# Strassen's scheme in the input projection of a hybrid decoder step: seven block products for eight, weight sums on GpSimd, product sums on VectorE

## The chip, the cores and the metric

The kernel runs on one core of a Trainium2 chip. The metric is the device time of one launch in microseconds (us). The core's engines work side by side, each with a queue of its own: TensorE (PE in the rows; PEld is its weight load), VectorE (DVE), ScalarE (ACT), GpSimd (POOL) and SyncE (SP), which issues nearly all transfers.

## The reference, cut to what matters

One step of two decoder layers for 512 prompt tokens and 32 sample tokens, 544 columns in all. The change touches one product, `z = hn @ w_in`; the rest is what its columns feed.

```python
for l in range(2):
    hn = rmsnorm(x, norm_g)
    z = hn @ w_in                      # (544 x 1024) @ (1024 x 10080), split into gates, heads, ...
    y_conv = c_b * conv3(c_c * c_h)                    # branch 0
    y_hg   = rmsnorm(hgrn2(hg_q, hg_f, hg_i, S0))      # branch 1
    y_mla  = mla(q_lat, kv_lat, k_pe, cache)           # branch 2
    y_mem  = cross_attention(m_q, mem_k, mem_v)        # branch 3
    ys = stack(y_conv, y_hg, y_mla, y_mem) * silu(sg)
    merged = sum_n sigmoid(mg[n]) * (ys[n] @ w_bout[n])
    x = x + merged @ w_o
```

All is float32. The large products are done as three products each of rounded parts (high x high, high x low, low x high), where low is what rounding left over.

## The kernel before, in words

**Tiles.** Activations stand feature-major: 128 features on the partitions, 544 token columns, eight such blocks for the 1024 features. The normalised input is split by `xn_finish` into `Hh` and `Hl` (8 blocks x 544 columns each). The columns of `w_in` are cut into 79 tiles of 128 a layer. One tile of weights is a 128x1024 array (512 KB): eight 128x128 blocks, one for each feature block.

**Items.** The program is a list of items: four for each of the memory key and value weights, the 79 tiles of `w_in` (the key says which: `mg` is a merge gate, `sg` a branch gate, `hq`, `hf`, `hi` the heads of hgrn2), the branch projections `pj` (32 a layer), and the output product `wo` (8). For each item:

- `load` (L1503) issues the transfer of the weights into a tile `wr` on SyncE, two items ahead (three buffers);
- `conv` (L1510) splits them one item ahead: ScalarE writes the high part `wh`, VectorE the low part `wl = wr - wh`;
- `z_mm` (L359) issues 48 matmuls: 8 blocks x 3 products for each half of 272 columns, summed in PSUM in one of two tiles `big` of two banks;
- `evac` reads the PSUM sum and makes of it what the branch needs (`ev_mg` at L662, `ev_pj` at L672 and others).

**Lanes.** Two generators run beside this: `lane_a` (memory attention, then hgrn2 of four heads) and `lane_b` (MLA of the prompt, then of eight samples). Each item makes one step of lane a after its first half and one of lane b at its end, so a lane's matmuls, its work on ScalarE and VectorE, and its gathers on GpSimd are spread over the items. They share 27 work tiles `t`, 128x544 each.

**What sets the order.** Instructions are written item by item, and a list scheduler with its own model of time puts them in order on each engine; each engine then works its queue strictly in that order and waits at the first instruction whose data or buffer isn't there. GpSimd's queue holds gathers of the paged cache (`in_lat`, `in_rop`), small copies, and the addition of a projection to the running sum (`e<-e`).

Of the kernel before, what the change touches and what calls it, by code (L numbers as in the profile page):

```python
# [19 lines left out]
P = 128  # L20
# [17 lines left out]
HG = ((2, 6), (0, 4))  # L38
NT = 27
PL = ()  # L40
PH = (2, 5)
LANE_PRI = {"a": 0, "b": 0, "mm": 0, "ev": 0, "cv": 0}
# [85 lines left out]

class Item:
    def __init__(self, key, l, src, n, mm, evac, pre=None):  # L130
        self.key, self.l, self.src, self.n = key, l, src, n
        self.mm, self.evac, self.pre = mm, evac, pre
        self.raw = self.hi = self.lo = None
# [3 lines left out]
def hybrid_kernel(ctx: ExitStack, tc: tile.TileContext, a, o):  # L137
# [5 lines left out]
    wrp = pool("wrp", 3)  # L143
    whp = pool("whp", 2)
    ep = pool("ep", 6)
# [4 lines left out]
    ssp = pool("ssp", 3)  # L150
    bigp = pool("bigp", 2, space=PSUM)
# [16 lines left out]
    big = lambda: bigp.tile([P, 2, 512], F32, tag="big", name="big")  # L168
# [45 lines left out]
    Rh = [kp.tile([P, 272], F32R, name=f"Rh{i}") for i in range(2)]  # L214
    Rl = [kp.tile([P, 272], F32R, name=f"Rl{i}") for i in range(2)]
# [21 lines left out]
    row4 = kp.tile([P, 4, P], F32R, name="row4")  # L237
    csq = kp.tile([P, T], F32, name="csq")

    def setup_first():  # L240
        V.memset(ones, 1.0)
        V.memset(epsc, EPS)
        x = t("b")[:, 0:4 * P].rearrange("p (h q) -> p h q", h=4)
        G.memset(x, 0.0)
        for h in range(4):
            G.memset(x[32 * h:32 * h + 1, h, :], 1.0)
        V.tensor_copy(row4, x)
        G.memset(cnew, 0.0)
        S.dma_start(out=gn, in_=a["gains"])

    def scale_rows(s1, s2):

        x = t("b")[:, 0:4 * NB]
        V.tensor_copy(x, row4i)
        ts(x, x, s1, s2, ALU.mult, ALU.add)
        V.tensor_copy(row4i, x)

    def setup():
        SY.dma_start(out=cst, in_=a["cst"])
        x = t("b")  # L260
# [98 lines left out]
    def z_mm(l, key):  # L359
        def run(it, half):  # L360
            if half == 0:
                it.ps = big()
            Hh, Hl = st[l]["H"]
            for k in range(KD):
                w = slice(k * P, (k + 1) * P)
                c = slice(half * HT, (half + 1) * HT)
                for n, (x, y) in enumerate(((it.hi, Hh), (it.hi, Hl), (it.lo, Hh))):
                    mm(it.ps[:, half, 0:HT], x[:, w], y[:, k, c], start=(k == 0 and n == 0), stop=(k == KD - 1 and n == 2))
        return run

    def proj_mm(l):
        def run(it, half):
            if half == 0:
                it.ps = big()
            yh, yl = st[l]["ys"]
            for k in range(4):
                w = slice(k * P, (k + 1) * P)
                c = slice(half * HT, (half + 1) * HT)
                for n, (x, y) in enumerate(((it.hi, yh), (it.hi, yl), (it.lo, yh))):
                    mm(it.ps[:, half, 0:HT], x[:, w], y[:, k, c], start=(k == 0 and n == 0), stop=(k == 3 and n == 2))  # L380
        return run

    def out_mm(l):
        def run(it, half):
            if half == 0:
                it.ps = big()
            Mh, Ml = st[l]["Ms"]
            if it.key[1] == 0:
                kh = [(k, hf) for k in range(KD) for hf in range(2)] if half == 0 else []
            else:  # L390
                kh = [(k, half) for k in range(KD)]
            for k, hf in kh:
                w = slice(k * P, (k + 1) * P)
                c = slice(hf * HT, (hf + 1) * HT)
                for n, (x, y) in enumerate(((it.hi, Mh), (it.hi, Ml), (it.lo, Mh))):
                    mm(it.ps[:, hf, 0:HT], x[:, w], y[:, k, c], start=(k == 0 and n == 0), stop=(k == KD - 1 and n == 2))
        return run

    def mem_mm(l, which, c):
        def run(it, half):  # L400
            if c == 0 and half == 0:
                st[l]["ps" + which] = big()
            it.ps = st[l]["ps" + which]
            mh, ml = st[l]["mn"]
            k = 2 * c + half
            w = slice(half * 512, (half + 1) * 512)
            for mt in range(2):
                m = slice((k % 2) * 256 + mt * P, (k % 2) * 256 + (mt + 1) * P)
                for n, (x, y) in enumerate(((mh, it.hi), (ml, it.hi), (mh, it.lo))):
                    mm(it.ps[:, mt, :], x[k // 2][:, m], y[:, w], start=(k == 0 and n == 0), stop=(k == KD - 1 and n == 2))  # L410
        return run

    def ps2(it):
        return it.ps[:, :, 0:HT]
# [17 lines left out]

    def xn_finish(l):
# [14 lines left out]
        Hh = kp.tile([P, KD, T], F32R, tag="H1", name="Hh")  # L448
        Hl = kp.tile([P, KD, T], F32R, tag="H2", name="Hl")
        st[l]["H"] = (Hh, Hl)  # L450
# [1219 lines left out]
```

## Time and profile before

| | |
|---|---|
| median of 3 runs | 1774.2 us (1771.57 to 1775.55) |
| the profiled execution | 1779.11 us |
| its span in the trace | 1777.3 us |
| TensorE busy | 1718.1 us, 14042 matmuls |
| VectorE busy | 1092.0 us, 2502 instructions |
| ScalarE busy | 863.9 us |
| GpSimd busy | 289.6 us |

Busy time of TensorE is the union of matmuls whose ends are modelled, so it hides short gaps between them; the spacing of matmuls in a dense stretch is the better measure. An instruction of VectorE is listed with its full duration, but the next one starts before it ends where neither waits, so start to start is what one costs in a full queue. Spans on GpSimd are rough. In the second layer the trace repeats the first nearly row by row.

### The profile page before, as it was taken

What the parts mean: (1) busy time and instruction counts of PE and PEld (TensorE: products, weight loads), DVE (VectorE), ACT (ScalarE), POOL (GpSimd) and SP (SyncE); (2) the same over time, 40 slices, a digit from 0 to 9 for tenths busy, and PEclk for the clock granted to TensorE, in tenths of its full rate; (3) what the DMA queues carried; (4) which work ended last, traced back from release to release, by engine and by line L of the source; (5) the groups of instructions that cost most, each with busy time, mean ns of one, the idle gap of its engine ahead of it and who ended that gap; (6) DMA issues with size and microseconds to landing.
All of it is one profiled execution on the core that took longest, in us unless ns stands there. A gap on an engine that the chain in (4) does not pass through costs nothing.

```text
span 1777.3 us, 36288 instructions
## 1 busy us (share of the span) xinstructions
PE 1718.1 (97%) x14042; PEld 1654.8 (93%) x14042; DVE 1092.0 (61%) x2502; ACT 863.9 (49%) x1659; POOL 289.6 (16%) x326
## 2 busy tenths in 40 slices
PE   6899999999998999999989999999999989999999
PEld 5899899999998999999969999999998989999999
DVE  7576554778676876334374656556877759753252
ACT  5646444565745663233246554356566465632231
POOL 3100000213232333100110100002131414221000
PEclk9999999999999999999989999999999989999999
DMA  6312632354344455433544235324444435554432
GB/s 225 116 60 69 208 111 83 121 158 152 112 148 140 142 173 158 145 128 108 158 142 123 60 122 187 98 72 152 151 127 140 155 92 171 169 152 145 147 108 99
DMA packets 129390, 236.79 MB, mean 133 GB/s; under 512 B 17025, under 2 KB 55298, under 8 KB 129218
## 3 DMA queue, kind: packets, MB, share of 16 engines
q1 hardware_dynamic: 121906, 213.45, 38.0%
q0 software_dynamic: 7168, 20.98, 4.0%
q8 instruction: 111, 1.82, 0.4%
q14 instruction: 61, 0.50, 0.1%
q10 hardware_dynamic: 144, 0.04, 0.0%
HBM read 204.55 MB, written 29.87 MB: 132 GB/s over the span
## 4 chain that ended last, share of the span: by engine, by line
PE 88%; ACT 5%; DVE 4%; issue 2%; DMA 1%; SPq 0%; DVEq 0%; ACTq 0%
PE big L171 67%; PE sm L171 19%; ACT L174 1%; ACT ta L174 1%; DVE wl L180 1%; ACT wh L174 1%; DVE e L177 1%; DVE ta L180 1%; ACT tb L174 1%; PE sm L1204 0%; PE sm L739 0%; PE sm L982 0%; DMA raw<-in_wk 0%; PE sm L1285 0%; PE sm L784 0%
## 5 line engine op out<-in xcount | busy, mean ns | idle before, releaser
L171 PE MATMUL big<-Hh,wh 128*128 128x272 f32 x2528 | 744.7, 295 | 4.2 <-ACT e L174 3.7
L171 PE MATMUL big<-Hh,wl 128*128 128x272 f32 x2528 | 739.2, 292 | 5.9 <-DVE wl L180 5.9
L171 PE MATMUL big<-Hl,wh 128*128 128x272 f32 x2528 | 734.4, 291 | 2.6 <-DVE Hl L180 2.6
L171 PEld LDWEIGHTS big<-Hh,wh 128*128 128x128 f32 x2528 | 478.9, 189 | 11.3 <-issue 4.6
L171 PEld LDWEIGHTS big<-Hh,wl 128*128 128x128 f32 x2528 | 478.1, 189 | 8.6 <-DVE wl L180 6.8
L171 PEld LDWEIGHTS big<-Hl,wh 128*128 128x128 f32 x2528 | 478.8, 189 | 7.3 <-DVE Hl L180 3.2
L174 ACT ACTIVATE wh<-wr 128x1024 fp32r<-128x1024 f32 (+1 forms) x248 | 235.0, 948 | 410.7 <-PE big L171 310.0
L180 DVE TENSOR_TENSOR wl<-wr,wh 128x1024 fp32r<-128x1024 f32 (+1 forms) x248 | 279.5, 1127 | 245.8 <-ACT wh L174 242.6
L174 ACT ACTIVATE tb<-sm 128x256 f32<-128x256 f32 (+6 forms) x380 | 137.1, 399 | 131.1 <-PE sm L171 100.1
L171 PE MATMUL big<-ysh,wl 128*128 128x272 f32 x512 | 148.3, 290 | 3.0 <-DVE wl L180 3.0
L171 PE MATMUL big<-ysh,wh 128*128 128x272 f32 x512 | 149.3, 292 | 0.0
L171 PE MATMUL big<-ysl,wh 128*128 128x272 f32 x512 | 148.6, 290 | 0.0
L180 DVE TENSOR_TENSOR ta<-ta 128x256 f32<-128x256 f32 (+3 forms) x248 | 110.0, 482 | 24.2 <-ACT ta L174 23.6
L171 PE MATMUL sm<-ta 128*128 128x128 f32 (+6 forms) x1424 | 124.4, 279 | 0.0
L174 ACT ACTIVATE ta<-ta 128x544 f32<-128x544 f32 (+3 forms) x180 | 94.8, 539 | 46.3 <-DVE ta L180 44.5
L171 PEld LDWEIGHTS sm<-ta 128*32 128x32 f32 (+1 forms) x1424 | 102.2, 147 | 8.8 <-issue 3.4
L171 PE MATMUL sm<-Rh,rb 128*128 128x272 f32 x512 | 109.7, 301 | 0.0
L189 DVE TENSOR_REDUCE s<-tb 128x8 f32<-128x512 f32 (+1 forms) x150 | 100.8, 673 | 13.2 <-ACT tb L174 12.9
L174 ACT ACTIVATE ta<-sm 128x512 f32<-128x512 f32 (+5 forms) x130 | 53.8, 429 | 99.3 <-PE sm L171 50.5
L171 PEld LDWEIGHTS big<-ysh,wl 128*128 128x128 f32 x512 | 96.4, 188 | 3.5 <-DVE wl L180 3.5
L180 POOL TENSOR_TENSOR e<-e 128x544 f32<-128x544 f32 x32 | 61.4, 1919 | 226.0 <-DVE e L177 186.9
L171 PEld LDWEIGHTS big<-ysh,wh 128*128 128x128 f32 x512 | 96.5, 189 | 1.0 <-issue 0.8
(236 smaller groups left out, 2564.8 us busy)
## 6 DMA issues: line engine op xcount, KB each, us to landing
wr<-in_w_in SPq DMA_DIRECT2D x158, 512.0 KB
wr<-in_wb SPq DMA_DIRECT2D x64, 256.0 KB
tb<-in_latT SPq DMA_DIRECT2D x256, 64.0 KB
md<-e SPq DMA_DIRECT2D x48, 272.0 KB
e<-md SPq DMA_DIRECT2D x32, 272.0 KB
ta<-in_mkT SPq DMA_DIRECT2D x32, 256.0 KB
ta<-in_mv SPq DMA_DIRECT2D x32, 256.0 KB
wr<-in_wo SPq DMA_DIRECT2D x16, 512.0 KB
```

The source lines that it names most:

```text
L171: return TE.matmul(out, lhsT, rhs, start=start, stop=stop)
L174: S.activation(out, in_, f, **k)
L177: V.scalar_tensor_tensor(out=out, in0=in0, scalar=sc, in1=in1, op0=op0, op1=op1)
L180: (eng or V).tensor_tensor(out=out, in0=in0, in1=in1, op=op)
L189: V.tensor_reduce(out=out, in_=in_, op=op, axis=AX.X, **k)
```

## The change

The 544 columns are cut in halves of 272, the 1024 features in halves of four blocks, and two tiles of weights are taken together, so that a pair is a product of 2x2 blocks. Strassen's scheme (in Winograd's form) makes it with seven block products. Each block product is 4 blocks x 3 products = 12 matmuls of 272 columns. 78 of a layer's 79 tiles go in 39 pairs; the tile `C` stays alone (`lone`).

- `xn_finish` writes seven blocks of the input (three as they are, four sums T1 to T4) in place of four: `Hh` and `Hl` grow from 8x544 to 7x4x272 columns.
- Of each pair's weights four blocks arrive by transfer (128x512 each), and **GpSimd** makes three more sums and one in place (`sums`, `after`): four additions of 128x512 a pair.
- All seven weight blocks are split into high and low, on ScalarE and VectorE as before, in pieces of 128x512 (`convert_to`).
- Each product lands in one PSUM bank of four. One is copied by ScalarE into a tile `uu`, and **VectorE** makes seven additions of 128x272 (PSUM plus SBUF into SBUF) that give the two results `z0`, `z1`. `evac` reads these from SBUF.
- Lane a steps after the second and the sixth product, lane b after the fourth and the seventh.
- Projections are read in halves (two instructions of 272 in place of one of 544). Loads run 11 block units ahead, sums 8, splits 4.
- To make room: 22 work tiles `t` for 27, 5 tiles `e` for 6, 2 softmax tiles `S` for 3, and smaller constants. The heads of hgrn2 start at other merge gates: `HG = ((2, 5), (0, 3))`.

```diff
-NT = 27
+HG = ((2, 5), (0, 3))
+NT = 22
-    wrp = pool("wrp", 3)
-    whp = pool("whp", 2)
-    ep = pool("ep", 6)
+    wrp = pool("wrp", 10)
+    whp = pool("whp", 4)
+    up = pool("up", 4)
+    ep = pool("ep", 5)
-    ssp = pool("ssp", 3)
-    bigp = pool("bigp", 2, space=PSUM)
+    ssp = pool("ssp", 2)
+    bigp = pool("bigp", 4, space=PSUM)
...
+    def three(u, out, rhs, first, last):
+        for k in range(4):
+            w = slice(k * P, (k + 1) * P)
+            yh, yl = rhs(k)
+            for n, (x, y) in enumerate(((u.hi, yh), (u.hi, yl), (u.lo, yh))):
+                mm(out, x[:, w], y, start=(first and k == 0 and n == 0), stop=(last and k == 3 and n == 2))
...
+    def pair(l, k0, k1, ev0, ev1, pre=None, psy=None):
+        def run(j):
+            def f(u):
+                ps = big()[:, 0:HT]
+                three(u, ps, block(l, (B11, B21, T2, T1, T3, B22, T4)[j]), True, True)
+                if j == 0:
+                    x["u"] = u_()
+                    act(x["u"], ps, AF.Copy)
+                elif j == 1:
+                    x["z0"] = ev0.alloc()
+                    tt(half0(x["z0"]), ps, x["u"], ALU.add)
+                    step("a")
+                elif j == 2:
+                    tt(x["u"], ps, x["u"], ALU.add)
+                elif j == 3:
+                    x["v"] = u_()
+                    tt(x["v"], ps, x["u"], ALU.add)
+                    step_b()
+                elif j == 4:
+                    x["z1"] = ev1.alloc()
+                    tt(half1(x["z1"]), ps, x["v"], ALU.add)
+                    tt(x["u"], ps, x["u"], ALU.add)
+                elif j == 5:
+                    z = x.pop("z0")
+                    tt(half1(z), ps, x.pop("v"), ALU.add)
+                    ev0(z, psy and psy(0))
+                    step("a")
+                else:
+                    z = x.pop("z1")
+                    tt(half0(z), ps, x.pop("u"), ALU.add)
+                    ev1(z, psy and psy(1))
+                    step_b()
...
+        def sums():
+            tt(us[3].raw, a21, a22, ALU.add, eng=G)
+            tt(us[2].raw, us[3].raw, a11, ALU.subtract, eng=G)
+            tt(a21, a11, a21, ALU.subtract, eng=G)
+        def after(u):
+            us[5].raw = u.raw
+            tt(u.raw, x.pop("a12"), u.raw, ALU.subtract, eng=G)
...
-        for d in range(KD):
-            h = e_()
-            stt(h, X[d], g_("norm", 8 * l + d), r, ALU.mult, ALU.mult)
-            act(Hh[:, d, :], h, AF.Copy)
-            tt(Hl[:, d, :], h, Hh[:, d, :].bitcast(F32), ALU.subtract, eng=G if d in PH else V)
+        for k in range(4):
+            h0, h1, x, y = e_(), e_(), e_(), e_()
+            stt(h0, X[k], g_("norm", 8 * l + k), r, ALU.mult, ALU.mult)
+            stt(h1, X[k + 4], g_("norm", 8 * l + k + 4), r, ALU.mult, ALU.mult)
+            tt(half0(x), half1(h0), half0(h0), ALU.subtract)
+            tt(half1(x), half1(h1), half0(x), ALU.subtract)
+            tt(half0(y), half1(h1), half1(h0), ALU.subtract, eng=G)
+            tt(half1(y), half0(h1), half1(x), ALU.subtract, eng=G)
...
+    for i, (it, u) in enumerate(units):
+        load_to(i + 11)
+        sum_to(i + 8)
+        convert_to(i + 4)
+        if it and it.pre:
+            it.pre()
+        u.run(u)
```

VectorE's queue of the kernel before, first layer, behind the fourth branch gate of hgrn2 (`wl` is a weight split, `big` the PSUM of a large product, the rest is lane b's sample attention):

```order
L180 TENSOR_TENSOR wl<-wr,wh 128x1024
L180 TENSOR_TENSOR s<-s 128x64
L1277 COPY S<-sm 128x16
L189 TENSOR_REDUCE s<-tb 128x8
L177 SCALAR_TENSOR_TENSOR s<-s 128x64
L189 TENSOR_REDUCE s<-tb 128x16
L177 SCALAR_TENSOR_TENSOR s<-s 128x64
L180 TENSOR_TENSOR rb<-tb,rb 128x512
L177 SCALAR_TENSOR_TENSOR e<-e,big 128x544
```

And in the changed kernel at the same gate (`uu` holds partial sums of products):

```order
L190 TENSOR_TENSOR uu<-big,uu 128x272
L190 TENSOR_TENSOR wl<-wr,wh 128x512
L1447 COPY S<-sm 128x16
L190 TENSOR_TENSOR S<-S,tb 128x256
L1447 COPY S<-sm 128x16
L190 TENSOR_TENSOR s<-s 128x64
L190 TENSOR_TENSOR e<-big,uu 128x272
L190 TENSOR_TENSOR uu<-big,uu 128x272
L190 TENSOR_TENSOR wl<-wr,wh 128x512
L190 TENSOR_TENSOR e<-big,uu 128x272
```

One split of 1024 columns among lane work has become splits of 512 with additions out of PSUM between them; the lane's instructions stand in the gaps.

GpSimd's queue of the kernel before, first layer, around the first merge additions `e<-e` of the memory branch:

```order
L915 MEMSET ta 128x544
L180 TENSOR_TENSOR e<-e 128x544
L1223 DMA tb<-in_lat,row4i 128x512 x2
L180 TENSOR_TENSOR e<-e 128x544
L1223 DMA tb<-in_rop,row4i 128x128 x4
```

And in the changed kernel:

```order
L1079 MEMSET ta 128x544
L190 TENSOR_TENSOR e<-e 128x544
L190 TENSOR_TENSOR wr<-wr 128x512 x4
L1391 DMA tb<-in_lat,row4i 128x512 x2
L190 TENSOR_TENSOR wr<-wr 128x512 x2
L190 TENSOR_TENSOR e<-e 128x544
L190 TENSOR_TENSOR wr<-wr 128x512
```

The weight sums `wr<-wr` of later pairs stand between the merge additions and the gathers, in one queue with them.

## Rows read from the trace of the kernel before

**Rows 1.** The page's first part: busy time (share of the span) and instructions.

```profile
PE 1718.1 (97%) x14042; PEld 1654.8 (93%) x14042; DVE 1092.0 (61%) x2502; ACT 863.9 (49%) x1659; POOL 289.6 (16%) x326
```

**Rows 2.** The chain that ended last, share of the span by engine.

```profile
PE 88%; ACT 5%; DVE 4%; issue 2%; DMA 1%; SPq 0%; DVEq 0%; ACTq 0%
```

**Rows 3.** The same chain in order of time, one piece: start, us, what.

```profile
153.99 6.03 PE big L171 x48
```

**Rows 4.** Groups by form: busy us, mean ns of one, idle before.

```profile
L171 PE MATMUL big<-Hh,wh 128*128 128x272 f32 x2528 | 744.7, 295 | 4.2 <-ACT e L174 3.7 <-ACT Hh L174 0.5
L174 ACT ACTIVATE wh<-wr 128x1024 fp32r<-128x1024 f32 x184 | 194.6, 1058 | 335.8 <-PE big L171 249.4 <-issue 73.0 <-DMA tb<-in_latT 7.5
L174 ACT ACTIVATE wh<-wr 128x512 fp32r<-128x512 f32 x64 | 40.4, 631 | 74.8 <-PE big L171 60.6 <-issue 13.2 <-ACT ta L174 1.0
L177 DVE SCALAR_TENSOR_TENSOR e<-e,sm 128x272 f32<-128x272 f32 x16 | 6.3, 434 | 0.6
```

**Rows 5.** Stretches, us: busy time of PE, PEld, DVE, ACT, POOL; clock, DMA, GB/s.

```profile
54.00:675.00 621.00, 607.91 (x5112) 584.93 (x5113) 418.75 (x1045) 343.40 (x695) 107.97 (x128) 0.99 0.42 129
675.00:945.00 270.00, 261.56 (x1989) 253.60 (x1988) 127.53 (x204) 89.91 (x136) 32.39 (x24) 0.97 0.45 142
945.00:1555.00 610.00, 596.63 (x5033) 573.29 (x5033) 413.45 (x1034) 340.35 (x690) 110.45 (x125) 0.99 0.41 128
1555.00:1777.00 222.00, 218.07 (x1770) 216.58 (x1768) 91.50 (x142) 59.83 (x89) 17.28 (x12) 1.00 0.41 130
540.00:585.00 45.00, 38.81 (x311) 37.99 (x310) 26.27 (x75) 28.36 (x53) 6.51 (x9) 0.92 0.36 112
585.00:630.00 45.00, 42.64 (x405) 41.82 (x404) 40.78 (x96) 24.14 (x58) 20.31 (x19) 1.00 0.55 163
```

**Rows 6.** The same first two stretches, matmuls that read the tile Hh alone.

```profile
54.00:675.00 621.00, 394.34 (x1926) 0.99 0.42 129
675.00:945.00 270.00, 125.36 (x653) 0.97 0.45 142
```

**Rows 7.** Groups by form within 360 to 405 us.

```profile
L180 DVE TENSOR_TENSOR wl<-wr,wh 128x1024 fp32r<-128x1024 f32 x5 | 6.1, 1217 | 1.6 <-ACT wh L174 1.6
L180 DVE TENSOR_TENSOR wl<-wr,wh 128x512 fp32r<-128x512 f32 x2 | 1.4, 690 | 0.9 <-ACT wh L174 0.9
```

**Rows 8.** Groups by form within 585 to 630 us.

```profile
L180 POOL TENSOR_TENSOR e<-e 128x544 f32<-128x544 f32 x4 | 6.9, 1728 | 31.2 <-DVE e L177 24.4 <-DVE S L1277 6.8
L180 DVE TENSOR_TENSOR wl<-wr,wh 128x1024 fp32r<-128x1024 f32 x4 | 6.0, 1496 | 0.3 <-ACT wh L174 0.2
L180 DVE TENSOR_TENSOR wl<-wr,wh 128x512 fp32r<-128x512 f32 x3 | 3.9, 1316 | 0.0
L180 POOL TENSOR_TENSOR ra<-ra,cst 96x512 fp32r<-96x512 f32 x2 | 2.0, 1038 | 2.7 <-DVE ra L180 2.7
```

**Rows 9.** VectorE in order of time: start us, us, what.

```profile
594.01 1.21 DVE L180 TENSOR_TENSOR wl<-wr,wh 128x1024 fp32r<-128x1024 f32 x1
595.14 0.41 DVE L180 TENSOR_TENSOR ta<-ta 128x256 f32<-128x256 f32 x1
595.48 0.42 DVE L180 TENSOR_TENSOR S<-S,sm 128x272 f32<-128x272 f32 x1
595.83 0.70 DVE L177 SCALAR_TENSOR_TENSOR e<-e,big 128x544 f32<-128x544 f32 x1
...
597.13 0.68 DVE L180 TENSOR_TENSOR wl<-wr,wh 128x512 fp32r<-128x512 f32 x1
597.73 0.41 DVE L180 TENSOR_TENSOR ta<-ta 128x256 f32<-128x256 f32 x1
```

**Rows 10.** GpSimd in order of time, two merge additions.

```profile
596.61 2.75 POOL L180 TENSOR_TENSOR e<-e 128x544 f32<-128x544 f32 x1 [6.40 <-DVE e L177]
...
623.28 1.35 POOL L180 TENSOR_TENSOR e<-e 128x544 f32<-128x544 f32 x1 [1.13 <-DVE e L177]
```

**Rows 11.** VectorE beside the second of them.

```profile
623.38 2.34 DVE L180 TENSOR_TENSOR wl<-wr,wh 128x1024 fp32r<-128x1024 f32 x1
```

More of the change, by code (lines that the diff above doesn't have):

```diff
@@ L356, in run_deferred @@
             fn()
[L359 to L411, printed above, removed]
@@ new lines, in outp, with run, f @@
+    def outp(l, d, ev):
+        it = Item()
+        out = []
+        def run(j):
+            def f(u):
+                Mh, Ml = st[l]["Ms"]
+                for hf in range(2):
+                    c = slice(hf * HT, (hf + 1) * HT)
+                    if j == 0:
+                        out.append(big()[:, 0:HT])
+                    three(u, out[hf], lambda k: (Mh[:, 4 * j + k, c], Ml[:, 4 * j + k, c]), j == 0, j == 1)
+                if j == 1:
+                    ev(out)
+                    out.clear()
+                    lane[0] = "a"
+                step("a") if j == 0 else step_b()
+            return f
+        plain(it, [a["wo"][l, d][:, 0:512], a["wo"][l, d][:, 512:1024]], run)
@@ new lines, in memp, with run, f @@
+    def memp(l, which, c, ev, pre=None):
+        it = Item()
+        def run(j):
+            def f(u):
+                mh, ml = st[l]["mn"]
+                k = 2 * c + j
+                if k == 0:
+                    st[l]["ps" + which] = [big(), big()]
+                out = st[l]["ps" + which]
+                for mt in range(2):
+                    m = slice((k % 2) * 256 + mt * P, (k % 2) * 256 + (mt + 1) * P)
+                    for n, (x, y) in enumerate(((mh, u.hi), (ml, u.hi), (mh, u.lo))):
+                        mm(out[mt], x[k // 2][:, m], y, start=(k == 0 and n == 0), stop=(k == KD - 1 and n == 2))
+                if k == KD - 1:
+                    ev(out)
+                    out.clear()
+                step("a") if j == 0 else step_b()
+            return f
+        w = a["w" + which][l, c]
+        plain(it, [w[:, 0:512], w[:, 512:1024]], run, pre)
@@ L672, in ev_pj, with run @@
     def ev_pj(l, n, d):
-        def run(it):
+        def run(pss):
             x = st[l].pop(("tm", d))
-            stt(v2(x), v2(x), 1.0, ps2(it), ALU.add, ALU.mult)
+            for ps, half in zip(pss, (half0, half1)):
+                stt(half(x), half(x), 1.0, ps, ALU.add, ALU.mult)
             if n != CONV:
@@ new lines, in hybrid_kernel, with load_to, sum_to @@
+    units = []
+    for it in items:
+        for n, u in enumerate(it.units):
+            units.append((it if n == 0 else None, u))
+    loaded, summed, converted = 0, 0, 0
+    def load_to(i):
+        nonlocal loaded
+        while loaded < min(i, len(units)):
+            it = units[loaded][0]
+            if it:
+                it.loads()
+            loaded += 1
+    def sum_to(i):
+        nonlocal summed
+        while summed < min(i, len(units)):
+            u = units[summed][1]
+            if u.sums:
+                u.sums()
+            summed += 1
```

569 lines of the change are left out of this document (318 added, 251 removed).

## The prediction

> **What bounds the kernel now.** I read the shares of the engines first, then the chain, then the stretches. TensorE is busy 97% of the span, VectorE 61%, ScalarE 49%, GpSimd 16% [rows 1]; the chain that ended last lies on TensorE for 88% [rows 2]. So TensorE bounds the kernel, and a matmul saved is time saved as long as nothing else becomes late. How near the others are is read from the stretches [rows 5]. Up to the end of hgrn2 and of the sample attention in each layer (54 to 675 us, 945 to 1555) VectorE is busy 418.75 and 413.45 us of 621 and 610, that is 68%. In the rest of each layer it is busy 127.53 of 270 and 91.50 of 222. In the densest 45 us (585 to 630) it reaches 40.78, that is 91%, and TensorE is down to 42.64 there. This is the margin that the change spends.
>
> **What it removes.** A pair took 96 matmuls of 272 columns and takes 84. In a dense stretch 48 of them last 6.03 us [rows 3], 0.1256 us each; the 295 ns of the group [rows 4] overlap and are no price. 12 x 0.1256 = 1.51 us a pair, and with 78 pairs 117.8 us. That is the whole gain. Where the pairs lie follows from the matmuls that read Hh, two of every three: 1926 and 653 in the first layer [rows 6], so 1926 x 1.5 / 96 = 30.1 pairs in the long stretch and 10.2 in the short one. The second layer has the rest of the 79 (the two lone tiles counted as one): I take 59.5 in the two long stretches and 19.5 in the two short ones.
>
> **What it adds on VectorE.** Prices are from start to start in a full queue [rows 9]: a split of 1024 columns 594.01 to 595.14, 1.13 us; a split of 512 597.13 to 597.73, 0.60; an instruction of 272 columns with one source in PSUM 595.48 to 595.83, 0.35 (it is listed with 0.43 [rows 4, 9]). A pair had two splits of 1024 and gets seven of 512: 7 x 0.60 - 2 x 1.13 = 1.94 us. Seven product sums are new: 7 x 0.35 = 2.45. Together 4.4 us a pair. Projections read in halves add some 5 us in all (160 instructions of 272 columns for 80 of 544, the price of one start each).
>
> **What it adds on ScalarE.** Seven splits for two, 7 x 0.631 - 2 x 1.058 = 2.3 us [rows 4], and a copy of 272 columns, under the 0.63 of 512: at most 2.9 us a pair, 226 us in all. ScalarE goes to 1090 us, some 60% of the span, so the rest of its time hides this; it costs nothing as long as it isn't made to wait.
>
> **What it adds on GpSimd, and what that takes from VectorE.** Four additions of 512 columns a pair, 312 in all. One of 544 that ran freely took 1.35 us [rows 10], so I estimate 1.27 by its columns, and 396 us in all; with 290 before, GpSimd stays under 40%. But it shares something with VectorE. Beside that addition of 1.35 us a split on VectorE took 2.34 us [rows 11], where the same takes 1.22 in a stretch without additions [rows 7]: it lost 1.12. Beside the other addition it was GpSimd that lost: 2.75 us [rows 10], and the split that VectorE ran then kept its 0.68 [rows 9]. So a weight sum costs VectorE between 0 and 1.12 us. Over 585 to 630 us, four merge additions and two of 96x512 cost the splits 4 x (1.496 - 1.217) + 3 x (1.316 - 0.690) = 3.0 us [rows 7, 8], or 0.5 for each addition; I take that, since VectorE is as full there as it will be everywhere. Four sums: 2.0 us a pair.
>
> [...]
>
> **The sum.** Long stretches: VectorE's 832.2 us grow by 59.5 x (4.4 + 2.0) = 381 to 1213 us, while TensorE's 1231 us shrink by 59.5 x 1.51 = 90 to 1141. So the bound passes to VectorE. How full its queue can be is the open factor: 91% is the most that the trace shows, 100% the limit; midway, 95%, gives 1277 us, 46 more than now. Short stretches: VectorE needs 219 + 19.5 x 6.4 = 344 of 492 us, TensorE stays the bound, and 19.5 x 1.51 = 29 us are saved. Start of a layer: `xn_finish` gains eight half sums and splits seven blocks in place of four, and the first product needs all four of its blocks; at 0.35 a half and 0.60 or so a split I count 8 us more of VectorE a layer. Memory matmuls run beside it; bounds 0 and 20 us a layer, and I take 5, so 10 in all. Five us for the halves. Smaller pools (22 work tiles for 27, 5 tiles e for 6) cost between nothing and what the lanes wait for a buffer, which the trace of before does not show; I take nothing, since a lane that is behind VectorE's queue waits for that first. So 46 - 29 + 10 + 5 = 32, less 2 for the lone tiles' share: 30 us. The profiled execution's 1779.11 us become 1809; it lies 4.9 above the median of 1774.2, so the forecast is 1804 us. With the queue 100% full it is -18 - 29 + 15 = -32, 1742 us; at 91% 1339 us in the long stretches, +94, 1868 us.
>
> **Rivals.**
>
> *TensorE stays the bound (faster).* GpSimd mostly loses, or the lookahead of four splits and four PSUM banks evens out the load. At no loss VectorE needs 832 + 59.5 x 4.4 = 1094 us, under TensorE's 1141. All 118 us would come in less the 15 of layer start and halves: 1671; with TensorE at 97% in the long stretches (1176) 1705. I put it at 1695. Against it: even then both queues would be over 92% full at once, each strictly in order. It decides where a sum costs under 0.37 us: (1245 x 0.95 - 1094) / 238 sums, 1245 being the time of the long stretches at which all comes out even.
>
> *Every weight sum makes VectorE wait in full.* At 1.12 us each, 8.9 us a pair: 1362 us in the long stretches, +131 - 29 + 15, 1891 us. For it: the lost 1.12 stands in the rows. Against it: the addition at 596.61 us, where GpSimd waited [rows 10].
>
> *Weight sums come late.* They stand in GpSimd's queue behind merge additions that wait for a projection (6.40 us of idle time before one [rows 10]) and ahead of gathers. Eight units ahead is 8 x 12 x 0.1256 = 12 us, which covers one such wait and not three. If the splits of each pair in the memory and hgrn2 branches waited 3 us, some 16 pairs would add 48 us: 1852. ScalarE would show it, stuck before a split `wh`.
>
> [...]
>
> **How the numbers follow.** Forecast 0.50, TensorE as the bound 0.32, full waits 0.07, late sums 0.07, clock 0.04. The forecast's own range is 1742 to 1868. About 0.05 of its 0.50 lies under 1770.6, and 0.05 within 0.2% of the time before, which is about what a measurement of this kernel can tell from no change; with 0.01 of the faster rival near it, 0.06. So faster 0.32 - 0.01 + 0.05 = 0.36, same 0.06, slower 0.58. The range that leaves out two in ten goes from 1690, into the faster rival, to 1868.
>
> **What would show it.** Right: in the long stretches VectorE busy over 90%, TensorE under 93%; long stretches of 1250 us or more in sum, short ones some 29 us less; splits of 512 whose mean is 0.2 to 0.4 us over 0.69; TensorE waiting for `big` to be read, or for `wl`. Wrong: splits at 0.69 to 0.75 in the mean (the sums cost nothing), TensorE at 97% still (the first rival), weight sums of 2 us or more that ScalarE waits for (late sums), or a granted clock under 0.95 in dense stretches. I am also wrong if the chain names a buffer of the lanes, which I priced at nothing.

## The result, and the profile after

The changed kernel takes 1934.2 us (median of 4 runs, 1930.75 to 1936.36) where the kernel before takes 1772.9 beside it: a ratio of 1.0906, with a 95% interval of 1.0883 to 1.0929. It is slower, as forecast, but by 161 us where the forecast had 30, and the time lies 66 us outside the range. The profiled execution spans 1933.8 us.

The page's first part after, as [rows 1], and the head of the chain, as [rows 2]:

```profile
PE 1710.7 (88%) x13106; PEld 1592.3 (82%) x13106; DVE 1666.1 (86%) x3577; ACT 1051.6 (54%) x2164; POOL 760.9 (39%) x642
```

```profile
PE 28%; DVE 18%; issue 4%; ACT 4%; DMA 1%; POOL 1%; SPq 0%; DVEq 0%; ACTq 0%; POOLq 0%
```

The 936 matmuls fewer stand there, yet TensorE's busy time fell by 7 us and not by 118: the granted clock is lower (0.948 in the mean, before 0.986), and matmuls that stand apart overlap less (one is listed with 0.30 us, and in a dense stretch they start 0.1256 us apart). TensorE stands idle for 223 us, before for 59: 114 us ahead of a lane's matmuls (before 15), 96 ahead of the large products (before 28), the rest at the start. The longest of these waits (who waited for whom: us in total, times, longest; before, the first two were 17.4 and 14.4 us):

```profile
PE big L181 <- DVE wl L190: 35.0, 38, 3.8
PE sm L181 <- DVE S L1447: 26.6, 18, 5.9
PE sm L1494 <- DVE m L199: 23.8, 9, 5.3
PE sm L1455 <- DVE S L1447: 18.2, 6, 6.0
PE big L181 <- DVE uu L190: 14.4, 15, 4.0
```

All five are for VectorE: `wl` is a weight split, `uu` a product sum, `S` and `m` are lane data. The part of the chain that could be followed back lies on TensorE and VectorE by turns.

The stretches that answer to the first four of [rows 5] (columns as there):

```profile
54.00:767.00 713.00, 624.57 (x4810) 574.24 (x4809) 637.55 (x1431) 415.42 (x885) 295.23 (x248) 0.93 0.37 114
767.00:1040.00 273.00, 254.41 (x1875) 241.71 (x1874) 221.44 (x395) 122.58 (x220) 94.68 (x71) 0.96 0.43 138
1040.00:1724.00 684.00, 597.04 (x4676) 552.43 (x4676) 608.54 (x1383) 401.98 (x859) 282.27 (x237) 0.95 0.37 116
1724.00:1934.00 210.00, 201.65 (x1622) 198.22 (x1620) 159.59 (x288) 82.11 (x147) 64.65 (x45) 1.00 0.40 130
```

The long stretches went from 1231 to 1397 us, the short ones from 492 to 483. In the long ones VectorE is busy 1246 us, 89%, TensorE 1222 us, 87%, and the granted clock is 0.93 and 0.95: neither queue is full.

The groups that answer to [rows 4] and [rows 8]:

```profile
L190 POOL TENSOR_TENSOR wr<-wr 128x512 f32<-128x512 f32 x312 | 466.7, 1503 | 688.7 <-DVE wl L190 300.9
L190 DVE TENSOR_TENSOR wl<-wr,wh 128x512 fp32r<-128x512 f32 x666 | 526.2, 795 | 65.2 <-ACT wh L184 57.9
L190 DVE TENSOR_TENSOR uu<-big,uu 128x272 f32<-128x272 f32 x234 | 100.3, 429 | 3.0 <-PE big L181 2.2
```

A weight sum lasts 1.50 us (estimated 1.27). The split lasts 0.795 in the mean, 0.105 over the undisturbed 0.69; the product sum, with one source in PSUM, its 0.43.

GpSimd and VectorE at one place in order of time (start us, us, what), as [rows 10, 11]:

```profile
169.92 2.58 POOL L190 TENSOR_TENSOR wr<-wr 128x512 f32<-128x512 f32 x2 [8.27 <-DVE wl L190]
172.44 0.19 POOL L759 COPY ncv<-us 128x16 f32<-128x16 f32 x1
172.59 2.54 POOL L190 TENSOR_TENSOR wr<-wr 128x512 f32<-128x512 f32 x2
```

```profile
171.28 1.25 DVE L187 SCALAR_TENSOR_TENSOR sl<-sl 128x17 f32<-128x17 f32 x1
172.45 0.68 DVE L199 TENSOR_REDUCE s<-sm 128x2 f32<-128x512 f32 x1
173.06 0.88 DVE L187 SCALAR_TENSOR_TENSOR e<-us,gn,e 128x32 f32<-128x32 f32 x1
173.86 1.35 DVE L190 TENSOR_TENSOR s<-s,sl 128x1 f32<-128x1 f32 x2
175.14 0.28 DVE L190 TENSOR_TENSOR Q<-Q,tb 96x128 f32<-96x128 f32 x1
175.34 0.42 DVE L190 TENSOR_TENSOR e<-big,uu 128x272 f32<-128x272 f32 x1
175.69 0.21 DVE L190 TENSOR_TENSOR s<-s,sl 128x1 f32<-128x1 f32 x2
```

Two additions of one column take 1.35 us while GpSimd adds and 0.21 right after it, so the stall falls on the smallest steps too. It doesn't fall on everything that VectorE does. Means in the changed kernel, beside those of e1 (below), which has no weight sums: the splits `wl<-wr,wh` 0.795 us for 0.713, the lanes' `ta<-ta` of 256 columns 0.570 for 0.439, the one-column additions `s<-s,sl` 0.227 for 0.158, the copies `S<-snew` 0.438 for 0.206; but the sums `uu<-big,uu` out of PSUM 0.429 for 0.432 and the reductions `s<-tb` of 512 columns 0.672 for 0.674. What doesn't fall on the splits falls mostly on the steps of the lanes.

The second loss shows in TensorE's order. Stretches of over 5 us in which only a lane's matmuls stand there, with no projection between them, sum to 43 us in the trace of before (the longest 16.7) and to 236 in the changed kernel (the longest 36.0). One lasts from 479.4 us for 35.0 us. TensorE, VectorE and ScalarE in it, where each waited:

```profile
499.41 0.58 PE L181 MATMUL sm<-cst,tb 128*128 128x16 f32 x2 [5.85 <-DVE S L1447]
...
502.69 1.10 PE L1455 MATMUL sm<-cst,tb 128*128 128x128 f32 x4
509.11 0.45 PE L1494 MATMUL sm<-cst,m 128*128 128x128 f32 x1 [5.32 <-DVE m L199]
```

```profile
493.60 0.17 DVE L1430 CAST Rl<-qal 128x16 fp32r<-128x16 f32 x1 [6.29 <-PE sm L181]
497.22 0.72 DVE L187 SCALAR_TENSOR_TENSOR ta<-ta 128x544 f32<-128x544 f32 x1 [3.44 <-ACT ta L184]
```

```profile
491.61 0.95 ACT L184 ACTIVATE ta<-sm,epsc 128x272 f32<-128x272 f32 x2 [0.82 <-PE sm L181]
492.58 1.28 ACT L184 ACT_TABLE_LOAD   x1
493.87 0.66 ACT L184 ACTIVATE ta<-ta 128x544 f32<-128x544 f32 x1
494.55 1.28 ACT L184 ACT_TABLE_LOAD   x1
495.84 0.66 ACT L184 ACTIVATE ta<-ta 128x544 f32<-128x544 f32 x1
```

No engine is short of time here: in these 35.0 us TensorE is busy 20.35, VectorE 21.25, ScalarE 16.30 and GpSimd 8.40, and the granted clock is 0.71. The end of an hgrn2 head goes from TensorE to ScalarE, through two table loads (1.28 us each), to VectorE; behind it in VectorE's queue stands what the other lane's next matmul needs, and TensorE has no projection in its order to put between. How long such stretches are doesn't by itself tell their cost: the run with the weight sums on VectorE (e2 below) has 303 us of them and is 24 us faster.

### The profile page after: what moved, and what is told of

Read it like the earlier page. It is cut to its first block, busy times and chain, and to the rows that moved or that the text cites. A ratio compares the mean times of both kernels' runs of the same rounds, so it can differ in the third digit from the quotient of the medians.

```text
span 1933.8 us, 37953 instructions
## 1 busy us (share of the span) xinstructions
PE 1710.7 (88%) x13106; PEld 1592.3 (82%) x13106; DVE 1666.1 (86%) x3577; ACT 1051.6 (54%) x2164; POOL 760.9 (39%) x642
## 4 chain that ended last, share of the span: by engine, by line
PE 28%; DVE 18%; issue 4%; ACT 4%; DMA 1%; POOL 1%; SPq 0%; DVEq 0%; ACTq 0%; POOLq 0%
PE big L181 22%; PE sm L181 6%; DVE wl L190 5%; DVE e L187 2%; DVE ta L190 2%; DVE e L190 1%; ACT ta L184 1%; ACT L184 1%; DVE s L199 1%; DVE ta L187 1%; DVE uu L190 1%; DMA wr<-in_w_in 1%; ACT wh L184 1%; DVE rb L190 1%; DVE s L190 1%
## 5 line engine op out<-in xcount | busy, mean ns | idle before, releaser
L181 PE MATMUL big<-H,wh 128*128 128x272 f32 x4944 | 1000.5, 297 | 44.8 <-DVE e L190 8.2
L181 PEld LDWEIGHTS big<-H,wh 128*128 128x128 f32 x4944 | 800.0, 192 | 73.0 <-issue 17.3
L181 PE MATMUL big<-H,wl 128*128 128x272 f32 x2472 | 734.0, 298 | 33.8 <-DVE wl L190 33.4
L190 POOL TENSOR_TENSOR wr<-wr 128x512 f32<-128x512 f32 x312 | 466.7, 1503 | 688.7 <-DVE wl L190 300.9
L184 ACT ACTIVATE wh<-wr 128x512 fp32r<-128x512 f32 x666 | 411.0, 627 | 344.8 <-PE big L181 296.6
L190 DVE TENSOR_TENSOR wl<-wr,wh 128x512 fp32r<-128x512 f32 x666 | 526.2, 795 | 65.2 <-ACT wh L184 57.9
L181 PEld LDWEIGHTS big<-H,wl 128*128 128x128 f32 x2472 | 474.7, 192 | 47.0 <-DVE wl L190 43.9
L184 ACT ACTIVATE ta<-ta 128x544 f32<-128x544 f32 (+4 forms) x204 | 107.7, 536 | 79.0 <-DVE ta L190 77.6
L181 PE MATMUL sm<-ta 128*128 128x128 f32 (+5 forms) x1424 | 137.3, 296 | 9.8 <-ACT ta L184 5.7
L190 DVE TENSOR_TENSOR uu<-big,uu 128x272 f32<-128x272 f32 x234 | 100.3, 429 | 3.0 <-PE big L181 2.2
```

The costliest lines, as they stand in the source:

```text
L181: return TE.matmul(out, lhsT, rhs, start=start, stop=stop)
L184: S.activation(out, in_, f, **k)
L190: (eng or V).tensor_tensor(out=out, in0=in0, in1=in1, op=op)
```

## Where the time lies

The experiments are read by one stage: from the first matmul of the convolution's projection (`big<-ysh`) to the first of hgrn2's. It holds 36 tiles of `w_in`, hgrn2's heads and most of the sample attention. In two parts, cut at the memory projection (in kernels with pairs the outer landmarks come one tile later, which leaves the sum alone), first layer: before, changed, fewer matmuls (f1), no sums (e4), no sums and own tiles (z1), and before with unused GpSimd additions (d2).

```profile
262.10:476.50 214.40, 214.40 (x1828) 210.31 (x1827) 146.77 (x353) 121.99 (x246) 37.37 (x43) 1.00 0.43 131
476.50:667.50 191.00, 178.38 (x1563) 175.34 (x1562) 141.97 (x346) 112.12 (x228) 59.15 (x57) 0.97 0.47 144
```

```profile
272.70:533.60 260.90, 225.46 (x1812) 210.12 (x1811) 223.53 (x526) 152.25 (x331) 101.56 (x81) 0.93 0.38 120
533.60:760.80 227.20, 188.69 (x1522) 177.98 (x1521) 200.78 (x456) 130.92 (x276) 107.92 (x92) 0.92 0.40 121
```

```profile
241.40:456.70 215.30, 204.87 (x1708) 199.65 (x1707) 147.80 (x356) 122.69 (x246) 36.73 (x43) 0.96 0.42 130
456.70:630.90 174.20, 163.92 (x1453) 160.66 (x1451) 139.03 (x327) 104.49 (x217) 60.93 (x55) 0.97 0.47 151
```

```profile
258.10:486.10 228.00, 210.25 (x1692) 201.94 (x1691) 167.98 (x414) 155.49 (x335) 36.53 (x42) 0.94 0.37 119
486.10:681.00 194.90, 176.00 (x1510) 169.98 (x1509) 158.63 (x391) 136.13 (x296) 65.11 (x57) 0.96 0.47 145
```

```profile
256.70:440.10 183.40, 183.40 (x1557) 178.51 (x1556) 143.31 (x332) 130.81 (x287) 28.93 (x28) 1.00 0.40 125
440.10:666.40 226.30, 191.33 (x1638) 185.11 (x1638) 181.31 (x471) 151.55 (x340) 73.83 (x70) 0.92 0.45 143
```

```profile
272.10:499.10 227.00, 218.49 (x1827) 211.34 (x1826) 165.13 (x351) 120.73 (x246) 101.87 (x85) 1.00 0.40 123
499.10:706.20 207.10, 186.24 (x1561) 181.42 (x1560) 158.88 (x341) 111.55 (x228) 92.74 (x83) 0.94 0.42 129
```

Over both layers, and the rest of the span (us of the profiled runs):

| kernel | hgrn2 stages | rest | span |
|---|---|---|---|
| before | 812 | 965 | 1777 |
| f1: before, 119 us of matmuls less | 778 | 912 | 1691 |
| z1: no sums, own tiles | 823 | 912 | 1735 |
| e4: no sums | 847 | 916 | 1763 |
| e1: no weight sums | 892 | 897 | 1789 |
| changed | 980 | 954 | 1934 |
| d2: before, unused additions | 868 | 984 | 1852 |
| h1: pairs in the MLA stage | 808 | 971 | 1779 |
| h2: pairs outside the hgrn2 stages | 859 | 933 | 1792 |

The whole loss lies in the hgrn2 stages: 168 us there, 11 won elsewhere. The MLA stage, which h1 and h2 speak of, is what follows them, from the first matmul of hgrn2's projection to the first of MLA's.

## The experiments

Theories as they stood in turn: A, VectorE is the bound and each GpSimd sum stops it; B, the lanes wait for the smaller pools; C, the sums come late; D, two strict queues with a short lookahead hold each other up; E, the order of TensorE; F, the lanes are a second path. A ratio is that to the kernel before on the same chip.

**e1, no weight sums.**

```diff
-            us[3].raw, us[2].raw = raw_(), raw_()
-            tt(us[3].raw, a21, a22, ALU.add, eng=G)    # and the other three
+            us[3].raw, us[2].raw = a21, a11
```

> The changed kernel without its four GpSimd weight sums a pair: products 2, 3 and 5 split A11, A21 and A12 as loaded instead, so the output is not the reference's; loads, splits, matmuls and product sums stay. Theory A (VectorE is the bound, and each GpSimd sum stops it by some 0.77 us, 241 us in all): VectorE's busy time falls from 1666 by about 240 us to some 1425, splits of 512 go to 0.68-0.70 us, TensorE becomes the bound again at over 93%, 1700 to 1760 us. Theory B (the lanes wait for the smaller pools): the waits stay, 1880 to 1930 us. [...]

Measured 1790.8 us, ratio 1.0085 (1.006 to 1.011). 143 us come back, but VectorE is still 82% busy and the kernel still slower than before:

```profile
PE 1655.3 (93%) x13106; PEld 1560.4 (87%) x13106; DVE 1460.5 (82%) x3577; ACT 1058.3 (59%) x2164; POOL 295.4 (17%) x330
```

VectorE lost 205.6 us, 0.66 for each of 312 sums: A as to the sums, though not all of its time.

**d1, the sums put back, for nobody.** On e1:

```diff
+            tt(junk, a21, a22, ALU.add, eng=G)         # four a pair, read by nobody
```

> The kernel without weight sums, with four GpSimd additions of 512 columns a pair put back that read the same loaded weights and write a scratch tile that nobody reads (so no split waits for them and they take no raw tiles; the output is not the reference's, as in the run without sums). Lock theory (a GpSimd addition stops VectorE's two-input instructions, whoever needs its result): VectorE's busy time goes back up from 1460 by some 180 to 240 us and the time from 1791 to 1890 to 1935 us. Lateness theory (splits wait for the sums, and the sums take raw tiles): stays at 1791 to 1815 us.

Measured 1953.1 us, 1.0985 (1.0955 to 1.1015).

```profile
PE 1719.2 (88%) x13106; PEld 1606.1 (82%) x13106; DVE 1678.8 (86%) x3577; ACT 1055.5 (54%) x2164; POOL 756.2 (39%) x642
```

162 us for additions whose results nothing waits for: the sums cost by stopping VectorE (0.70 us each here), and C falls. That it takes 19 us more than the changed kernel, with one raw tile less, is not explained.

**d2, the same in the kernel before.**

```diff
+            tt(junk, it.raw[:, 0:512], it.raw[:, 512:1024], ALU.add, eng=G)   # two a tile
```

> The kernel before with two such unused GpSimd additions of 512 columns beside each tile of the input projection, 316 in all, and 25 work tiles for 27; nothing left out, no Strassen. If 0.77 us of stall a sum is a price that holds anywhere, VectorE goes from 1091 to some 1330 us busy, 75%. If only a full VectorE costs time: 1775 to 1795 us, TensorE still at 96%. If the stalls reach TensorE through the lanes long before VectorE is full: 1820 us or more.

Measured 1857.3 us, 1.046 (1.0439 to 1.0481).

```profile
PE 1740.6 (94%) x14042; PEld 1666.7 (90%) x14042; DVE 1237.7 (67%) x2502; ACT 863.0 (47%) x1659; POOL 740.7 (40%) x642
```

Here a sum costs VectorE (1237.7 - 1092.0) / 316 = 0.46 us, near the forecast's own price. But with 146 us of stalls come 81 us of time while VectorE is 67% busy and has no other work added. So the time does not go by how full VectorE is. The run also has 25 work tiles for 27 (24 cost 5 us in e5), and its additions wait 666 us in GpSimd's queue for the transfers of their weights, with the lanes' gathers behind them. TensorE's own waits for GpSimd are 5.5 us in all, so gathers that come late are not the main part; how much of the 81 us they are is not shown.

**f2, each sum in two halves.**

```diff
+                for c in (slice(0, 256), slice(256, 512)):
+                    tt(out[:, c], p[:, c], q[:, c], op, eng=G)
```

> The changed kernel with each of its GpSimd weight sums as two of 256 columns; nothing left out, 624 sums of half the length. If GpSimd holds VectorE off for the length of its instruction: the stall of each is about half, some 0.4 us, the sum of the stalls stays near 240 to 280 us, and the time at 1900 to 1960 us, a little better at most, since VectorE gets in between. If the stall is a price per instruction: twice as much in all, over 2050 us.

Measured 1930.3 us, 1.0873 (1.0853 to 1.0893), VectorE busy 1629.0 us: 168.5 over e1, 0.27 for each of 624. The stall goes by length, not by number (in the changed kernel 0.66 for each of 312, twice as long). VectorE had 37 us less to do than in the changed kernel; the time fell by 4 us, which the intervals don't tell from nothing.

**e2, the sums on VectorE.** `eng=G` taken out of the four lines.

> The changed kernel with all 312 weight sums on VectorE in place of GpSimd, nothing left out. 312 x 0.60 us = 187 us more work on VectorE. Theory A (a GpSimd sum costs VectorE 0.77 us): the stall of 241 us goes and 187 us of work comes, so VectorE's busy time ends some 50 us lower, at 1610 to 1630, and the time is 1870 to 1930 us: no slower than with GpSimd. [...]

Measured 1910.1 us, 1.0759 (1.0733 to 1.0786), VectorE busy 1634.4: nearly as A said. An addition costs VectorE nearly the same whether it makes it (173.9 us over e1, 0.56 each) or is stopped by it (0.66). This run also answers a rival, that the sums cost by holding up the gathers behind them in GpSimd's queue: here none stands there, and each us more on VectorE than in e1 still costs 0.69 us of time, as in the changed kernel (143 us for 205.6, 0.70).

**e3, no product sums.**

```diff
-                    tt(half0(x["z0"]), ps, x["u"], ALU.add)
+                    act(half0(x["z0"]), ps, AF.Copy)   # four copies a pair, the other sums gone
```

> The changed kernel without its seven product sums a pair on VectorE: four products are copied by ScalarE into the halves of the two output tiles, the other three are computed and never read, so the output is not the reference's; weight sums, splits and all 84 matmuls stay. Theory A: VectorE loses 78 x 7 x 0.35 = 191 us, of which 59.5/78 = 146 in the long stretches; at the 89% to which its queue was full, 164 us: 1770 us (1740 to 1800), VectorE still at 85% or so of the long stretches, since the GpSimd sums still stop it. Theory B: above 1880 us. Theory C: the late sums stay as late, above 1850 us.

Measured 1877.2 us, 1.0558 (1.0528 to 1.0588): a miss for A, and in the range of C, against which d1 speaks. VectorE lost 169 us of work and the time only 57; with VectorE at 80% the kernel is far slower than before. The edit gives ScalarE 71 us more, and VectorE now waits 144 us for it before splits, so part of the gain may be lost there.

**e4, neither.** Both edits.

> The changed kernel without the weight sums and without the product sums (the edits of the two runs without one of them, together; the output is not the reference's). What is left of the change: 84 matmuls a pair for 96, seven splits of 512 for two of 1024, blocks of 272 columns, the smaller pools, the start of a layer. Theory A (the bound is VectorE's work): VectorE falls to 1666 - 206 - 169 = 1290 us busy, under 75%, TensorE is the bound at 96% or more, 1680 to 1710 us. Theory D (the two queues hold each other up, each strictly in order with a lookahead of four splits of 1.5 us; work taken off VectorE comes back only in part): the gains add up as they stood alone, 143 and 57 us, to 1735 us (1720 to 1760), TensorE at 94 to 95%.

Measured 1763.1 us, 0.9936 (0.9919 to 0.9952). A is refuted as the whole cause: VectorE is 73% busy, TensorE has 118 us less to do, and 11 come in. D had 1735.

**e5, e6, e7: pools, lookahead, grain.** The kernel before with smaller pools (`NT = 24`, `ep` 5, `ssp` 2); the changed kernel with `whp` 5, `wrp` 8, `convert_to(i + 5)`, `load_to(i + 10)`; the kernel before with `cuts` giving two halves for every tile of 1024.

> The kernel before with smaller pools, near those of the change: 24 work tiles for 27 (the change has 22), 5 tiles e for 6, 2 tiles for the start for 3; nothing else differs and nothing is left out. Theory A: within 0.5% of the kernel before, 1765 to 1782 us. Theory B (the lanes wait for buffers): over 1800 us.

> The changed kernel, nothing left out, with the splits five units ahead of the matmuls instead of four (5 tiles each of wh and wl for 4); to make room 8 raw tiles for 10, loads ten units ahead for eleven. No engine has more or less to do. Theory A (VectorE's work is the bound): 1920 to 1950 us, no change. Theory D (the short lookahead holds TensorE up whenever VectorE is some us behind): 1870 to 1905 us, a granted clock over 0.955 in the mean, and fewer waits of TensorE for wl. If the raw tiles are what is short, slower: over 1950.

> The kernel before with every split of 1024 columns made as two of 512, on ScalarE and on VectorE; nothing left out. VectorE gets 160 x (2 x 0.60 - 1.13) = 11 us more, ScalarE 160 x (2 x 0.631 - 1.058) = 33 us. If only the work counts: 1770 to 1785 us. If it is the finer grain of the splits that costs the changed kernel its time: over 1800 us.

Measured 1780.0 us, 1.0027 (1.0015 to 1.004); 1920.5, 1.0827 (1.0807 to 1.0847); 1773.1, 0.9994 (0.9984 to 1.0004). Pools cost the old kernel 5 us, a fifth unit of lookahead wins some 14 of 160, the grain costs nothing. So B and D are not the main causes as far as these runs go: the change has 22 work tiles where e5 has 24, and e6 paid for its lookahead with two raw tiles.

**o1 to o4, every matmul kept in the order of the code,** in the changed kernel, e4, the kernel before and the mix h1.

```diff
-        return TE.matmul(out, lhsT, rhs, start=start, stop=stop)
+        return tc.keep_in_program_order(TE.matmul(out, lhsT, rhs, start=start, stop=stop))
```

> The changed kernel with one edit: every matmul keeps on TensorE the place that it has in the code, so that a lane's matmuls stand between two block products instead of in runs of 95 to 124 lane matmuls with no product between them (the scheduler's order has five such runs over 60, the kernel before none). Work, pools and sums are the same. Theory E (the order: in the changed kernel TensorE spends 587 us in stretches of lane matmuls alone, before 479, since a lane's own chain of waits is laid bare there and the clock falls): about 100 us come back, 1820 to 1860 us. [...] If lane data come too late for places in the code, slower than 1960.

> The same edit in the kernel without weight sums and product sums (the output is not the reference's). Theory E: what held that kernel at 1763 us with VectorE at 73% were its runs of lane matmuls (543 us in such stretches against 479 before; one of 41.5 us, with gaps of 5.9 and 5.3 us); with them broken up 1680 to 1705 us, TensorE at 96% or more. If something else of the change holds it (the start of a layer, blocks of 272): 1740 to 1770.

> The kernel before with the same edit, nothing left out: what the edit does by itself. Theory E: it has no runs of lane matmuls over 60 to break up, so 1765 to 1790 us; slower than that only if lane matmuls stand in the code ahead of their data, and then by waits of TensorE for sm.

> The mix (pairs in the MLA stages alone, weight sums on VectorE, nothing left out) with the same edit. It lost 14 to 19 us at the start of each layer and won 13 in each MLA stage. Theory E: its lane runs (481 us) are no longer than those before, so the order gives little: 1765 to 1780 us, as the kernel before under the same edit less 0 to 10 us. If the order costs time at the layer starts: 1745 to 1760.

Measured 2151.5 us (1.2123, 1.2097 to 1.2149), 1969.0 (1.108, 1.1056 to 1.1105), 2017.8 (1.1364, 1.1337 to 1.139) and 2028.0 (1.1424, 1.1401 to 1.1447). Theory E missed in all four; in o1 and o3 the case came that their expectations set against it, lane data too late for their places in the code. (They count no stretch of over 60 lane matmuls in the kernel before; its trace has two long ones of 79, at 545.0 and 1424.1 us.) Breaking up the runs in this way makes every kernel slower, the one before by 244 us. What TensorE waited for most in o3 (line waited for, us in total, times, longest):

```profile
PE sm L171 <- DVE S L1277: 91.7, 40, 6.8
PE sm L1285 <- DVE S L1277: 29.4, 14, 6.3
```

In the code's order TensorE meets lane steps before their data are there, and it stood idle for 202 us ahead of lane matmuls, 15 in the kernel before. The edit is too coarse to acquit the order of the change, but it shows how much lane latency that order has to hide.

**z1, tiles of their own for hgrn2's inputs,** on e4.

```diff
+    zp = pool("zp", 5)
...
-        @ev(ta)
+        @ev(lambda: zp.tile([P, T], F32, tag="z", name="z"))
```

> The kernel without weight sums and product sums (the output is not the reference's), with five tiles of their own for the outputs hq, hf and hi of the hgrn2 heads, which otherwise take one of the 22 work tiles that the lanes share (room: 6 raw tiles for 10, loads 8 units ahead, 1 tile uu). The runs of 125 and 106 lane matmuls on TensorE, which stood behind the pair (hq, hf) of the third and fourth head, are gone from the order; one of 179 at the start of the hgrn2 gates takes the place of that of 69. Theory F (the lanes: a pair's output waits for a work tile that a head of hgrn2 still holds, and TensorE then runs through lane steps at their latency): the stage from the first memory gate to the first hgrn2 gate, 10 pairs, goes from 228 to 200-208 us, and the whole from 1763 to 1705-1735 us. If the lanes are simply too slow for the shorter stages, whoever holds the tiles: what is won there is lost at the hgrn2 gates, 1755 to 1775 us.

Measured 1736.9 us, 0.978 (0.9762 to 0.9799). The first part of the stage falls by 45 us, and TensorE is busy without a gap in it; the second takes back 31. The time lies between the expectation's two cases, just above the first, and each explains a part: the pair's outputs do wait for work tiles, and what the first part wins is in good part lost in the second, where TensorE waits for the lanes.

**f1, the saving alone.**

```diff
+                    if n == 2 and k < 3:
+                        continue
```

> The kernel before with 6 of the 48 matmuls of each tile of the input projection left out (the low part of the weights in the first three of eight blocks; the output loses that correction), and nothing added: 158 x 6 x 0.1256 = 119 us less for TensorE, as much as the seven products save. It shows what the saving was worth at most. If TensorE alone had set the time: 1655 us (to 1670). Theory F (the lanes of hgrn2 and of the sample attention are a second path almost as long in their stages): the two hgrn2 stages of a layer give back only a part of their 27 us, 1680 to 1720 us.

Measured 1692.4 us, 0.9528 (0.951 to 0.9547): 82 of 119 us. The first part of the stage took 215.3 us for 214.4, with one matmul in fifteen gone, nothing added and VectorE at 69%. All the idle time of TensorE in it, 10.4 us, stands in one stretch of lane matmuls, from 420 to 439 us, and the granted clock is 0.96:

```profile
423.53 0.30 PE L1326 MATMUL sm<-cst,m 128*128 128x128 f32 x1 [3.49 <-DVE m L189]
...
426.22 0.82 PE L171 MATMUL sm<-Rh,rb 128*128 128x272 f32 x2 [1.47 <-ACT tb L174]
...
435.14 1.97 PE L171 MATMUL sm<-QR,tb 128*128 128x64 f32 x8 [5.09 <-DVE S L1279]
```

That fits F: there the lanes' steps, one behind the other over three engines, take as long as TensorE's work did, and a shorter projection leaves them bare. Whether another order on TensorE, or one more tile for a result, would have put projection matmuls in between is not shown; z1 says that in the changed kernel tiles have a part in it.

**h1, h2: pairs only in some stages,** with weight sums on VectorE; elsewhere `two(...)`, which calls `lone` twice.

```diff
-                    pair(l, ("mg", n, d), ...)
+                    (pair if n == MLA else two)(l, ("mg", n, d), ...)
```

> A mix, nothing left out: pairs of seven products only for the gates of the MLA stage of each layer (12 tiles, where VectorE was busy under 60%), with their weight sums on VectorE; all other tiles by the change's function for a single tile (48 matmuls each, two splits of 512, two sums of 272 from PSUM, no weight sum). In those stages the run with the sums on VectorE took 138 us against 153 before, so 2 x 15 = 30 us of gain; the other stages keep TensorE as the bound (VectorE gets 1.5 us for two tiles more than before, some 90 us in the long stretches, 75%), the layer start costs 10 us and the smaller pools 5. Theory A and D alike: 1755 us (1745 to 1770), a little faster than before. If blocks of 272 columns, small pools and the layer start by themselves hold TensorE up, 1785 us or more.

> Pairs of seven products for the first 22 tiles of each layer (from the latents to the convolution's gates) and for the 12 of the MLA stage; single tiles in the stages in which hgrn2 runs; weight sums on VectorE; nothing left out. By the run with all sums on VectorE the first stage wins 10.6 us a layer and the MLA stage 8.7 (each with the tile by which the landmark moved taken off), and the single tiles of the mix kept the hgrn2 stages at their old time: 1774 - 2 x 19 = 1736 us (1725 to 1755), faster than both kernels. If the lanes then lag at the hgrn2 stages, what the first stage wins is given back there: 1770 us or more.

Measured 1777.7 us, 1.0018 (1.0008 to 1.0028), and 1792.6, 1.0082 (1.0058 to 1.0106). h1 lies between its two cases; h2 missed its forecast and came out as its second case, lanes that lag. h1 won some 7 us in each MLA stage and lost 13 and 8 ahead of the convolution's projection, where a layer starts (the tile by which the landmarks move taken off). h2 won 32 us outside the hgrn2 stages and lost 46 in them, though they have single tiles as in h1, where they took no longer than before. That fits lanes that arrive late because the stage ahead went by faster; no run shows it directly. No version computed the whole reference faster than the kernel before.

## Why the prediction was wrong, step by step

- **"That is the whole gain", 117.8 us.** The count was right, the worth was not: f1 shows 82 at most. [rows 2] showed a chain on TensorE, which doesn't tell how near the next path is. A sign was in view: the stretch from 540 us in [rows 5] holds a wait that is a lane's, the one wait of weight between 476 and 667 us in the kernel before:

```profile
PE sm L171 <- DVE S L1277: 7.0, 2, 6.2
```

- **VectorE's added work.** 574 us measured, some 520 forecast for the whole (78 x 6.4, 16 and 5). Product sums: 169 us for 546, 0.31 each for 0.35. Weight sums: 0.66 for 0.5, within the bounds of 0 to 1.12. The stall was priced from splits alone [rows 7, 8]; on them it is 0.105 in the mean, where 0.2 to 0.4 was expected. Against e1, whose splits take 0.713, they lost 55 of the 206 us; the rest fell on other instructions, most of them the lanes'.
- **The step that failed: "how full its queue can be", 95%.** The long stretches were to take VectorE's 1213 us divided by 0.95, 1277. VectorE's work came to 1246, 33 off; the time came to 1397, at 89%, below the 91% taken as the worst. VectorE isn't a bound that work is divided by: d2 loses 81 us at 67%, and e4 at 73% wins 11 of 118. In place of the divisor the runs show that work on VectorE costs time long before its queue is full: 0.56 us for each us added in d2, and against e1 0.69 in e2, 0.70 in the changed kernel and 0.74 in d1 (less in e3, 0.34, which gives ScalarE more to do), and that TensorE, mostly for VectorE's results, waits both ahead of the lanes' matmuls (114 us, before 15) and of the large products (96, before 28). That the lanes are a second path nearly as long as TensorE's is read from f1 and z1; it isn't shown apart from the order of the queues and the tiles.
- **Short stretches, 29 us won:** 9. **Start of a layer, 10 us:** h1 lost 21 in the two layers, within the bounds of 0 to 40. **Smaller pools, nothing:** 5 us in the kernel before, some 26 with the pairs' outputs in the same tiles (e4 to z1).
- **ScalarE and GpSimd hidden:** 188 us more on ScalarE and GpSimd at 39%, as forecast.
- **Rivals.** TensorE as the bound (1695) needed free sums; with no sums at all it is 1763. Full waits (1891) came nearest to the time, by luck: a sum cost 0.66 us and not 1.12. Late sums: refuted by d1; ScalarE waited 21 us for them. The clock fell to 0.948 in the mean (before 0.986), 4% of TensorE's 1711 us or some 65, an estimate from these numbers; in the stretches of both traces a clock under 0.97 comes with waits (0.92 in [rows 5]; 0.93, 0.95 and 0.96 above), and no run shows what it costs apart from them. The prediction gave it a chance of 0.04 as a case by itself instead of adding it to every forecast in which TensorE waits.
- **Its own signs.** Of those for being right, TensorE under 93% (87) and long stretches of over 1250 us (1397) came, and waits for `wl` and for `big` to be read (35.0 and 14.4 us); VectorE over 90% (89), the 29 us and the splits did not. Of those for being wrong, a granted clock under 0.95 came in the first long stretch (0.93), beside waits.

In a row, against the kernel before: 82 us won by fewer matmuls (f1), 44 lost by what else z1 has of the change, 26 by shared tiles (e4), 171 by the sums of both kinds; that makes 159 of the 161. What stays open: how the 44 us between f1 and z1 divide between the layer start, the copies, the finer splits and the other start of the hgrn2 heads.

## What to carry to other kernels

A bound at 97% tells what the next us saved there is worth, not the hundredth: take the saving out alone first (f1, 82 of 119 us), and see what is left to win. Where lanes of small dependent steps fill the gaps of a bound engine, look for the longest one and count its latency as a path of its own; work added to an engine that is two thirds busy can then cost time (d2, 81 us at 67%). The GpSimd additions here were paid by VectorE, nearly as if it made them itself (0.66 us each for 0.56).

## What the runs showed of the hardware

- A GpSimd addition stops even a VectorE instruction of one column: 1.35 us for two that take 0.21 right after it (changed kernel, from 173.86 and 175.69 us); 0.227 in the mean of 80, 0.158 without weight sums (e1).
- One 512-column addition on GpSimd cost VectorE 0.46 us in the kernel that keeps it 67% busy (d2), 0.66 and 0.70 in the two at 86% (the changed kernel, d1); one of 256 columns 0.27 (f2).
- VectorE sums with a source in PSUM kept 0.43 us beside them (0.429; 0.432 without any weight sums, e1), and reductions of 512 columns their 0.67 (0.672; 0.674).
- TensorE waits at the next matmul in its order until the data are there: 202 us of idle time ahead of lane matmuls in the code's order (o3), 15 in the scheduler's (the kernel before).
